# Strassen's seven products for three of the four gate pairs of the last branch

## The chip, the cores and the metric

The kernel runs on one core of a Trainium2 chip. The time is that of one execution in device microseconds; the figure of a kernel is the median of its runs. Matmuls run on TensorE (PE), which has an instruction stream of its own for loading weights (PEld); VectorE (DVE), ScalarE (ACT) and GpSimd (POOL) do the elementwise work, and SyncE (SP) issues the transfers.

## The reference

Two layers of a decoder trunk on x of 512 tokens by 1024 columns, float32. What matters here is the end of a layer:

```python
def hybrid_layer(x, ...):
    h = rms_norm(x, norm_g)
    proj = h @ w_in                      # (512, 1024) @ (1024, IN_COLS)
    ...                                  # three branches a, c, r, each (512, 512)
    g = jax.nn.sigmoid(gates).reshape(b, s, 3, 1024)
    merged = g[:, :, 0] * (a @ w_branch[0])
    merged = merged + g[:, :, 1] * (c @ w_branch[1])
    merged = merged + g[:, :, 2] * (r @ w_branch[2])
    return x + merged @ w_out
```

`gates` are the last 3 x 1024 columns of `proj`. The second layer is followed by a last RMSNorm.

## The kernel before

Everything is kept transposed: 128 features on the partitions, the 512 tokens along a row. The normalised input h is 8 such tiles, each as a high and a low part in a reduced float32 format (`split`, L196 to L198: ACT copies the high part on L197, DVE or POOL subtracts for the low part on L194). A product of full precision is three matmuls (`mm3`, L200 to L203: high by high L201, high by low L202, low by high L203).

Weights come as chunks of 128 x 1024 (512 KB), in an order fixed on the host (`chunk_order`). SP loads them into `wraw`, which has three buffers (L214); `split_next` splits a chunk into `whi` and `wlo` (three buffers each), ACT both halves, the low part of the first half on DVE and of the second on POOL. One chunk is split ahead of the one PE is using (`LOOK = 1`).

PE's order is that of the program text; the order of the other engines is set by a scheduler when the kernel is built. In the text, work that waits for other engines is put off by a count of `tick`s (`at(lag, fn)`), so that score blocks of attention and retention fall between projections.

`merge(br, parts, jp, first, final)` makes two of the 8 tiles of `merged` for one branch: one W chunk of the branch's weights and two gate chunks. For each of the two tiles `proj` makes the gate (8 weight tiles x 3 = 24 matmuls of 512 columns) and ACT its tanh (L489), then W gives 12 matmuls of 512 columns, DVE multiplies (L649, with the product in PSUM) and adds to the running sum m, a tile called xm (L650). For the last branch (`br == 2`, retention) the sum is split into `vm`, the operand of the output projection `out_proj`, whose first two output tiles take the operands 0 to 5 before the others. SP also reloads x into the buffers of xm (`xm<-xT`, `xm<-xsave`).

Retention runs between the merges of branch 0: `rk` and `rq` are rotated with the tables in the tile `tab` (L445 to L449), their low parts `qk` made on L461, a score block's diagonal multiplied by a triangle on L534, the block split into `st`, and PE multiplies it with the values (pa<-st,vm).

Of the kernel before, what the change touches and what calls it, by code (L numbers as in the profile page):

```python
# [38 lines left out]

def merge_chunks(br, jp):
    c = GATE + br * D + jp * 256
    return [("W", br, jp), ("A", c), ("A", c + P)]


# [26 lines left out]
    return L  # L73


def rot_perm(base):


    idx = []
    for h in range(4):  # L80
        for ihi in range(2):
            for half in range(2):
                for ilo in range(16):
                    idx.append(base + h * 64 + half * 32 + ihi * 16 + ilo)
    return idx


def lay_weights(w_in, w_branch, w_out):
    cols = np.arange(w_in.shape[2])
    cols[RQ:RQ + 256] = rot_perm(RQ)  # L90
    cols[RK:RK + 256] = rot_perm(RK)
    out = []
    for l in range(DEPTH):
        for c in chunk_order(l):
            if c[0] == "B":
                a = w_in[l][c[2] * 256:(c[2] + 1) * 256, c[1]:c[1] + 512].reshape(2, P, 512)
            elif c[0] == "A":
                a = w_in[l][:, cols[c[1]:c[1] + P]].reshape(8, P, P)
            elif c[0] == "W":
                a = w_branch[l, c[1]][:, c[2] * 256:(c[2] + 1) * 256].reshape(4, P, 256)  # L100
            else:
                a = w_out[l][:, c[1] * P:(c[1] + 1) * P].reshape(8, P, P)
            out.append(a.transpose(1, 0, 2).reshape(P, 1024))
    return np.stack(out)
# [50 lines left out]
def tile_hybrid_trunk(ctx: ExitStack, tc: tile.TileContext, xT, w, prm, lam, tab, cmat, outT):  # L155
# [29 lines left out]
    def pj():  # L185
        return ps.tile([P, S], F32, tag="pj", bufs=NPJ, name="pj")
# [16 lines left out]
        T.matmul(out, wl, xh, start=False, stop=stop)  # L203


    order = [(l, c) for l in range(DEPTH) for c in chunk_order(l)]
    pos = [0]
    raws, parts = [], []

    def prefetch():  # L210
        i = pos[0] + len(parts) + len(raws)
        if i < len(order):
            raw = t("wraw", 3, (P, 1024))
            nc.sync.dma_start(raw, w[i])  # L214
            raws.append(raw)

    def split_next():
        if not raws:
            prefetch()
        if raws:  # L220
            raw = raws.pop(0)
            l, c = order[pos[0] + len(parts)]
            off = 0 if c[0] == "O" and l == DEPTH - 1 else WOFF
            hi, lo = (tr(tag, 3, (P, WPITCH))[:, off:off + 1024] for tag in ("whi", "wlo"))
            for c in range(0, 1024, 512):
                c = slice(c, c + 512)
                if pos[0] or parts or c.start:
                    split(hi[:, c], lo[:, c], raw[:, c], G if c.start else V)
                else:
                    V.tensor_copy(hi[:, c], raw[:, c])  # L230
                    lo_part(lo[:, c], raw[:, c], hi[:, c])
            parts.append((hi, lo))

    def chunk(l, *key):

# [128 lines left out]
    for l in range(DEPTH):  # L364
# [269 lines left out]
        def merge(br, parts, jp, first, final):  # L634
            wh, wl = chunk(l, "W", br, jp)
            for i in range(2):
# [14 lines left out]
                if final:  # L651
                    hi, lo = tr("vm", 16), tr("vm", 16)
                    split(hi, lo, m[j])
                    mp[j] = (hi, lo)

        def attention(p):
            qk, o, wt = attn_qk(p), {}, {}
            for s in range(8):
                at(AOFF + ARATE * s, lambda s=s: attn_step(2 * p + s // 4, s % 4, o, wt, qk))
            for i in range(2):  # L660
                az[2 * p + i] = silu_proj(AZ + 256 * p + P * i)
# [12 lines left out]
        for jp in range(4):  # L674
            rz[jp] = silu_proj(RZ + P * jp)
            merge(0, abr, jp, False, False)
        assert len(abr) == 4 and len(rbr) == 4 and not todo, (len(abr), len(rbr), len(todo))
        for jp in range(4):
            merge(2, rbr, jp, False, True)


        x2 = []
# [80 lines left out]
```

## Time and profile before

| | before |
|---|---|
| median of 3 runs | 1064.31 us (1064.06 to 1064.67) |
| the profiled execution, its own time | 1063.46 us |
| its span, first to last instruction | 1061.7 us |
| mean granted clock of TensorE | 0.997 |
| busy PE / DVE / ACT / POOL | 1050.7 / 681.7 / 502.9 / 319.2 us |
| three last merge pairs of branch 2, layer 0 and 1 | 48.96 and 48.65 us |

The rows of the profile carry the line numbers of the kernel before. "Idle before" is the time in which an engine did nothing ahead of an instruction, with what ended it. Durations of neighbouring instructions on an engine overlap a little, so that the distance of starts is the better measure of the pace.

### The profile page before, as it was taken

What the parts mean: (1) busy time and instruction counts of PE and PEld (TensorE: products, weight loads), DVE (VectorE), ACT (ScalarE), POOL (GpSimd) and SP (SyncE); (2) the same over time, 40 slices, a digit from 0 to 9 for tenths busy, and PEclk for the clock granted to TensorE, in tenths of its full rate; (3) what the DMA queues carried; (4) which work ended last, traced back from release to release, by engine and by line L of the source; (5) the groups of instructions that cost most, each with busy time, mean ns of one, the idle gap of its engine ahead of it and who ended that gap; (6) DMA issues with size and microseconds to landing.
All of it is one profiled execution on the core that took longest, in us unless ns stands there. A gap on an engine that the chain in (4) does not pass through costs nothing.

```text
span 1061.7 us, 13847 instructions
## 1 busy us (share of the span) xinstructions
PE 1050.7 (99%) x5010; PEld 878.8 (83%) x5010; DVE 681.7 (64%) x1168; ACT 502.9 (47%) x942; POOL 319.2 (30%) x254
## 2 busy tenths in 40 slices
PE   8999999999999999999999999999999999999997
PEld 6888888888888888888888888888888888888896
DVE  7687686765677566345528776868546956654454
ACT  6454454543554555334434535545345545544343
POOL 6222233221233333232422222232112333332264
PEclk9999999999999999999999999999999999999998
DMA  6322222232234222444422232223313432134363
GB/s 253 107 96 99 84 76 86 93 119 80 80 119 139 66 91 79 132 129 146 143 100 90 80 119 79 81 80 108 111 61 100 135 100 78 65 107 132 110 208 121
DMA packets 34340, 113.57 MB, mean 107 GB/s; under 512 B 3936, under 2 KB 4064, under 8 KB 34272
## 3 DMA queue, kind: packets, MB, share of 16 engines
q1 hardware_dynamic: 34128, 112.44, 32.6%
q8 instruction: 39, 0.64, 0.2%
q14 instruction: 29, 0.24, 0.1%
q10 hardware_dynamic: 144, 0.26, 0.1%
HBM read 108.49 MB, written 4.19 MB: 106 GB/s over the span
## 4 chain that ended last, share of the span: by engine, by line
PE 92%; DVE 5%; ACT 1%; issue 1%; DMA 0%; SPq 0%; DVEq 0%; ACTq 0%
PE pj L201 28%; PE pj L203 28%; PE pj L202 28%; PE pa L479 3%; PE pa L203 1%; PE pa L202 1%; DVE wa L427 1%; PE pa L201 1%; DVE wlo L194 1%; PE pa L605 1%; DVE h L194 1%; DVE vm L395 1%; ACT h L197 1%; DMA xm<-xT 0%; DVE xb L375 0%
## 5 line engine op out<-in xcount | busy, mean ns | idle before, releaser
L194 POOL TENSOR_TENSOR wlo<-wraw,whi 128x512 fp32r<-128x512 f32 x184 | 252.1, 1372 | 626.6 <-ACT whi L197 584.5
L201 PE MATMUL pj<-h,whi 128*128 128x512 f32 x960 | 379.4, 395 | 0.0
L203 PE MATMUL pj<-h,wlo 128*128 128x512 f32 x960 | 374.9, 390 | 0.0
L202 PE MATMUL pj<-h,whi 128*128 128x512 f32 x960 | 374.3, 390 | 0.2
L197 ACT CAST whi<-wraw 128x512 fp32r<-128x512 f32 x367 | 216.4, 618 | 219.2 <-PE pj L202 144.8
L194 DVE TENSOR_TENSOR wlo<-wraw,whi 128x512 fp32r<-128x512 f32 x184 | 153.9, 837 | 125.4 <-ACT whi L197 124.3
L203 PEld LDWEIGHTS pj<-h,wlo 128*128 128x128 f32 x960 | 180.2, 188 | 39.3 <-DVE wlo L194 0.5
L202 PEld LDWEIGHTS pj<-h,whi 128*128 128x128 f32 x960 | 180.5, 188 | 35.7 <-DVE h L194 1.1
L201 PEld LDWEIGHTS pj<-h,whi 128*128 128x128 f32 x960 | 180.4, 188 | 35.0
L201 PE MATMUL pj<-xb,whi 128*128 128x512 f32 x192 | 75.1, 391 | 0.0
L203 PE MATMUL pj<-xb,wlo 128*128 128x512 f32 x192 | 74.8, 390 | 0.0
L202 PE MATMUL pj<-xb,whi 128*128 128x512 f32 x192 | 74.7, 389 | 0.0
L592 ACT ACTIVATE p<-pa,nm 128x128 f32<-128x128 f32 (+3 forms) x64 | 33.5, 526 | 69.0 <-DVE nm L589 68.8
L516 DVE RECIPROCAL e<-e 128x512 f32<-128x512 f32 x16 | 53.6, 3350 | 18.0 <-ACT e L515 18.0
L197 ACT CAST st<-pa 128x256 fp32r<-128x256 f32 (+2 forms) x80 | 29.7, 372 | 70.2 <-DVE pa L534 40.5
L201 PE MATMUL pj<-vm,whi 128*128 128x256 f32 (+1 forms) x192 | 60.5, 315 | 0.0
L202 PE MATMUL pj<-vm,whi 128*128 128x256 f32 (+1 forms) x192 | 60.4, 315 | 0.0
L203 PE MATMUL pj<-vm,wlo 128*128 128x256 f32 (+1 forms) x192 | 60.3, 314 | 0.0
L649 DVE SCALAR_TENSOR_TENSOR wb<-wa,pj 128x512 f32<-128x512 f32 x32 | 22.0, 687 | 41.8 <-PE pj L203 38.6
L194 DVE TENSOR_TENSOR st<-pa,st 128x256 fp32r<-128x256 f32 (+2 forms) x80 | 33.7, 421 | 17.0 <-ACT st L197 16.4
L203 PEld LDWEIGHTS pj<-xb,wlo 128*128 128x128 f32 x192 | 36.0, 188 | 7.6
L202 PEld LDWEIGHTS pj<-xb,whi 128*128 128x128 f32 x192 | 36.1, 188 | 7.2
(132 smaller groups left out, 1428.8 us busy)
## 6 DMA issues: line engine op xcount, KB each, us to landing
wraw<-w SPq DMA_DIRECT2D x183, 512.0 KB, 3.4
tab<-tab SPq DMA_DIRECT2D x10, 512.0 KB, 3.4
xm<-xT SPq DMA_DIRECT2D x15, 256.0 KB, 3.6
xsave<-xm SPq DMA_DIRECT2D x8, 256.0 KB, 2.1
xm<-xsave SPq DMA_DIRECT2D x8, 256.0 KB, 2.8
outT<-p SPq DMA_DIRECT2D x8, 256.0 KB, 2.1
wraw<-w SPq DMA_DIRECT2D x2, 256.0 KB, 3.3
xm<-xT ACTq DMA_DIRECT2D x1, 256.0 KB, 3.0
```

The source lines that it names most:

```text
L194: eng.tensor_tensor(lo, x, hi, op=ALU.subtract)
L197: A.copy(hi, x)
L201: T.matmul(out, wh, xh, start=start, stop=False)
L202: T.matmul(out, wh, xl, start=False, stop=False)
L203: T.matmul(out, wl, xh, start=False, stop=stop)
L395: V.scalar_tensor_tensor(lo, banks[tt], rtok[:, tt:tt + 1], hi, op0=ALU.mult, op1=ALU.subtract)
L427: V.scalar_tensor_tensor(hk, x[k], ng[k], rrow, op0=ALU.mult, op1=ALU.mult)
L479: T.matmul(o, ac[i][:, asl], bc[i][:, bsl], start=i == 0, stop=i == 1)
L516: V.reciprocal(r, r)
L592: A.activation(pc[:, :n], sp[:, :n], AF.Exp, bias=nm, scale=0.125, accum_out=sm)
L605: T.transpose(tp[:, j * P:(j + 1) * P], p1[:, j * P:(j + 1) * P], ident)
L649: V.scalar_tensor_tensor(y, g, 1.0, o, op0=ALU.add, op1=ALU.mult)
```

## The change

For branch 2 the pairs jp = 1, 2, 3 are made by `merge_fast`; jp = 0 stays as it was. The two gate tiles of a pair are a product of 2 x 2 blocks: two weight chunks a and b (128 gate columns each, each of two halves of 512, which are 4 of the 8 feature tiles), by h of two halves of features and two halves of tokens (LF and RT, 256 each). Instead of 8 products of quarters there are 7, in Winograd's form of Strassen's scheme, each of 4 feature tiles x 3 matmuls of 256 columns. It needs four sums of weights (`sources`: s1 = b0 + b1, s2 = s1 - a0, a0 - b0, a1 - s2; three on POOL, s2 on DVE), four sums of h (`h_sums` and `late_sums`, once in a layer, for kk = 0 to 3, with two 512-wide sums on POOL into the single buffer `tab`, four 256-wide ones on DVE, and two more splits), and seven additions of results on DVE instead of none (`add`), with one ACT copy out of PSUM. A pair's two chunks are used as four parts ("F"), which hold 3.5 x 1024 columns instead of 2 x 1024. `h_sums(0)` stands in the program behind the second merge of branch 0, the other three and `late_sums` ahead of the first merge of branch 2.

```diff
--- before.py
+++ after.py
@@ -39,8 +39,15 @@
 
 
 
+def fast(br, jp):
+    return br == 2 and jp > 0
 def merge_chunks(br, jp):
     c = GATE + br * D + jp * 256
+    if fast(br, jp):
+        return [("F", c), ("F", c + P), ("W", br, jp)]
     return [("W", br, jp), ("A", c), ("A", c + P)]
 
 
@@ -73,6 +80,18 @@
     return L
 
 
+def part_order(layer):
+    L, C = [], iter(chunk_order(layer))
+    for c in C:
+        if c[0] == "F":
+            next(C)
+            L += [("F", c[1], i) for i in range(4)]
+        else:
+            L.append(c)
+    return L
 def rot_perm(base):
 
 
...
@@ -203,33 +222,63 @@
         T.matmul(out, wl, xh, start=False, stop=stop)
 
 
-    order = [(l, c) for l in range(DEPTH) for c in chunk_order(l)]
-    pos = [0]
-    raws, parts = [], []
+    order = [(l, c) for l in range(DEPTH) for c in part_order(l)]
+    nchunks = sum(len(chunk_order(l)) for l in range(DEPTH))
+    pos, loaded = [0], [1]
+    raws, parts, fp = [], [], {}
 
     def prefetch():
-        i = pos[0] + len(parts) + len(raws)
-        if i < len(order):
+        if loaded[0] < nchunks:
             raw = t("wraw", 3, (P, 1024))
-            nc.sync.dma_start(raw, w[i])
+            nc.sync.dma_start(raw, w[loaded[0]])
+            loaded[0] += 1
             raws.append(raw)
 
-    def split_next():
+    def next_raw():
         if not raws:
             prefetch()
-        if raws:
-            raw = raws.pop(0)
-            l, c = order[pos[0] + len(parts)]
-            off = 0 if c[0] == "O" and l == DEPTH - 1 else WOFF
-            hi, lo = (tr(tag, 3, (P, WPITCH))[:, off:off + 1024] for tag in ("whi", "wlo"))
-            for c in range(0, 1024, 512):
-                c = slice(c, c + 512)
-                if pos[0] or parts or c.start:
-                    split(hi[:, c], lo[:, c], raw[:, c], G if c.start else V)
-                else:
-                    V.tensor_copy(hi[:, c], raw[:, c])
-                    lo_part(lo[:, c], raw[:, c], hi[:, c])
-            parts.append((hi, lo))
+        return raws.pop(0)
+    def sources(c):
+        if c[0] != "F":
+            raw = next_raw()
+            return [raw[:, 0:512], raw[:, 512:1024]]
+        if c[2] == 0:
+            ra, rb = next_raw(), next_raw()
+            fp["a"], fp["b"] = [[r[:, 0:512], r[:, 512:1024]] for r in (ra, rb)]
+        (a0, a1), (b0, b1) = fp["a"], fp["b"]
+        if c[2] == 0:
+            s1 = fp["s1"] = t("wc", 1)
+            G.tensor_tensor(s1, b0, b1, op=ALU.add)
+            return [a0, s1]
+        if c[2] == 1:
+            s2 = fp["s2"] = t("sq", 1)
+            V.tensor_tensor(s2, fp["s1"], a0, op=ALU.subtract)
+            return [a1, s2]
+        if c[2] == 2:
+            G.tensor_tensor(b0, a0, b0, op=ALU.subtract)
+            G.tensor_tensor(a1, a1, fp["s2"], op=ALU.subtract)
+            return [b0, a1]
+        return [b1]
+    def split_next():
+        n = pos[0] + len(parts)
+        if n == len(order):
+            return
+        l, c = order[n]
+        off = 0 if c[0] == "F" or c[0] == "O" and l == DEPTH - 1 else WOFF
+        src = sources(c)
+        hi, lo = (tr(tag, 3, (P, WPITCH))[:, off:off + 1024] for tag in ("whi", "wlo"))
+        for i, raw in enumerate(src):
+            c = slice(i * 512, i * 512 + 512)
+            if n or i:
+                split(hi[:, c], lo[:, c], raw, G if i else V)
+            else:
+                V.tensor_copy(hi[:, c], raw)
+                lo_part(lo[:, c], raw, hi[:, c])
+        parts.append((hi, lo))
 
     def chunk(l, *key):
 
@@ -653,6 +702,86 @@
                     split(hi, lo, m[j])
                     mp[j] = (hi, lo)
 
+        LF, RT = slice(0, 256), slice(256, 512)
+        hs, late = {}, {}
+        def h_sums(kk):
+            uv = t("tab", 1, (P, 2 * S))
+            u, v = uv[:, 0:S], uv[:, S:2 * S]
+            G.tensor_tensor(u, h[kk][0], h[kk][1], op=ALU.add)
+            G.tensor_tensor(v, h[4 + kk][0], h[4 + kk][1], op=ALU.add)
+            a, b = t("wc", 1), t(f"p{kk % 2}", 2)
+            V.tensor_tensor(a[:, LF], u[:, RT], u[:, LF], op=ALU.subtract)
+            V.tensor_tensor(a[:, RT], v[:, RT], a[:, LF], op=ALU.subtract)
+            V.tensor_tensor(b[:, LF], v[:, RT], u[:, RT], op=ALU.subtract)
+            V.tensor_tensor(b[:, RT], v[:, LF], a[:, RT], op=ALU.subtract)
+            hi, lo = tr("qk", 8), tr("qk", 8)
+            split(hi, lo, a)
+            hs[1, kk], hs[2, kk] = [(hi[:, s], lo[:, s]) for s in (LF, RT)]
+            late[kk] = b
+        def late_sums(kk):
+            hi, lo = tr("xb", 16), tr("xb", 16)
+            split(hi, lo, late[kk])
+            hs[3, kk], hs[4, kk] = [(hi[:, s], lo[:, s]) for s in (LF, RT)]
+        def quarter(o, part, i, mov):
+            for kk in range(4):
+                c = slice(i * 512 + kk * P, i * 512 + (kk + 1) * P)
+                mm3(o, part[0][:, c], part[1][:, c], *mov(kk), kk == 0, kk == 3)
+        def hq(k0, s):
+            return lambda kk: (h[k0 + kk][0][:, s], h[k0 + kk][1][:, s])
+        def ht(n):
+            return lambda kk: hs[n, kk]
+        def merge_fast(br, parts, jp):
+            c = GATE + br * D + jp * 256
+            ga, gb = t("ez", 4), t("ez", 4)
+            def quarters(n, moving):
+                p, o = chunk(l, "F", c, n), pa()
+                for i, mov in enumerate(moving):
+                    quarter(o[:, i * 256:(i + 1) * 256], p, i, mov)
+                return o[:, LF], o[:, RT]
+            def add(out, prod, other):
+                V.tensor_tensor(out, prod, other, op=ALU.add)
+            q1, q5 = quarters(0, (hq(0, LF), ht(1)))
+            A.copy(ga[:, LF], q1)
+            q2, q6 = quarters(1, (hq(4, LF), ht(2)))
+            u2 = t("e1", 1)
+            add(u2[:, LF], q6, ga[:, LF])
+            add(ga[:, LF], q2, ga[:, LF])
+            add(ga[:, RT], q5, u2[:, LF])
+            q7, q3 = quarters(2, (ht(3), hq(4, RT)))
+            add(gb[:, LF], q7, u2[:, LF])
+            add(ga[:, RT], q3, ga[:, RT])
+            tanh_half(ga, ga)
+            add(gb[:, RT], q5, gb[:, LF])
+            q4, _ = quarters(3, (ht(4),))
+            add(gb[:, LF], q4, gb[:, LF])
+            tanh_half(gb, gb)
+            wh, wl = chunk(l, "W", br, jp)
+            for i, g in enumerate((ga, gb)):
+                j, o = 2 * jp + i, pj()
+                for k in range(4):
+                    cs = slice(k * 256 + i * P, k * 256 + (i + 1) * P)
+                    mm3(o, wh[:, cs], wl[:, cs], parts[k][0], parts[k][1], k == 0, k == 3)
+                y = t("wb", 1)
+                V.scalar_tensor_tensor(y, g, 1.0, o, op0=ALU.add, op1=ALU.mult)
+                V.tensor_tensor(m[j], m[j], y, op=ALU.add)
+                hi, lo = tr("vm", 16), tr("vm", 16)
+                split(hi, lo, m[j])
+                mp[j] = (hi, lo)
         def attention(p):
             qk, o, wt = attn_qk(p), {}, {}
             for s in range(8):
@@ -674,9 +803,16 @@
         for jp in range(4):
             rz[jp] = silu_proj(RZ + P * jp)
             merge(0, abr, jp, False, False)
+            if jp == 1:
+                h_sums(0)
         assert len(abr) == 4 and len(rbr) == 4 and not todo, (len(abr), len(rbr), len(todo))
-        for jp in range(4):
-            merge(2, rbr, jp, False, True)
+        for kk in range(1, 4):
+            h_sums(kk)
+        for kk in range(4):
+            late_sums(kk)
+        merge(2, rbr, 0, False, True)
+        for jp in range(1, 4):
+            merge_fast(2, rbr, jp)
 
 
         x2 = []
```

In the order of the built kernels PE has 5161 rows instead of 4945, DVE 1120 instead of 1016 and POOL 180 instead of 124.

The first place is the start of retention in a layer, on DVE. Before (L461 makes qk's low parts, L534 is the triangle of a score block, `cm` holds the triangle, L649 and L650 belong to the merge of branch 0):

```order
L447 TENSOR_TENSOR wa<-pj,tab 128x512
L194 TENSOR_TENSOR wlo<-wraw,whi 128x512
L449 TENSOR_TENSOR wa<-wa,wb 128x512
L493 SCALAR_TENSOR_TENSOR ez<-ez,pj 128x512
L461 TENSOR_TENSOR qk<-wa,qk 64x512 x2
L194 TENSOR_TENSOR wlo<-wraw,whi 128x512
L534 TENSOR_TENSOR pa<-pa,cm 128x128
L194 TENSOR_TENSOR st<-pa,st 128x512
L649 SCALAR_TENSOR_TENSOR wb<-wa,pj 128x512
```

After the change the same stretch reads so (L496 is L447 of before, L510 L461, L542 L493, L583 L534; `p_3409` is the tile b of `h_sums(0)`, `p_3844` that of `h_sums(1)`, L718 to L721 are their four sums):

```order
L496 TENSOR_TENSOR wa<-pj,tab 128x512
L213 TENSOR_TENSOR wlo<-wraw,whi 128x512
L498 TENSOR_TENSOR wa<-wa,wb 128x512
L718 TENSOR_TENSOR wc<-tab 128x256
L720 TENSOR_TENSOR p_3409<-tab 128x256
L719 TENSOR_TENSOR wc<-tab,wc 128x256
L542 SCALAR_TENSOR_TENSOR ez<-ez,pj 128x512
L510 TENSOR_TENSOR qk<-wa,qk 64x512 x2
L721 TENSOR_TENSOR p_3409<-tab,wc 128x256
L720 TENSOR_TENSOR p_3844<-tab 128x256
L583 TENSOR_TENSOR pa<-pa,cm 128x128
L213 TENSOR_TENSOR wlo<-wraw,whi 128x512
```

Seven instructions more stand between L496 and the first triangle L583, the last of them L720 of the second chunk; a chunk's low part that stood ahead of the triangle now stands behind it.

POOL at the same place after the change, where L715 and L716 write `tab` for a chunk of h each and the other rows are second halves of weight chunks (before, only those were there):

```order
L213 TENSOR_TENSOR wlo<-wraw,whi 128x512
L715 TENSOR_TENSOR tab<-h 128x512
L716 TENSOR_TENSOR tab<-h 128x512
L213 TENSOR_TENSOR wlo<-wraw,whi 128x512
L715 TENSOR_TENSOR tab<-h 128x512
L716 TENSOR_TENSOR tab<-h 128x512
```

The two pairs of sums have one low part between them.

In a fast pair (the second of a layer) DVE has this after the change, where `sq<-wc,wraw` (L258) is s2 of the pair that follows, L755 are the additions of this pair, `wlo` the low parts of coming parts, L779 and L780 the merge (L649 and L650 before):

```order
L213 TENSOR_TENSOR wlo<-wraw,whi 128x512
L258 TENSOR_TENSOR sq<-wc,wraw 128x512
L755 TENSOR_TENSOR ez<-pa,e_4267 128x256
L755 TENSOR_TENSOR ez<-pa,ez 128x256 x2
L213 TENSOR_TENSOR wlo<-wraw,whi 128x512
L755 TENSOR_TENSOR ez<-pa,ez 128x256
L213 TENSOR_TENSOR wlo<-wraw,whi 128x512
L779 SCALAR_TENSOR_TENSOR wb<-ez,pj 128x512
L780 TENSOR_TENSOR xm<-xm,wb 128x512
L213 TENSOR_TENSOR vm<-xm,vm 128x512
L779 SCALAR_TENSOR_TENSOR wb<-ez,pj 128x512
```

L258 stands behind this pair's first three additions and ahead of its other four.

## Rows read from the trace of the kernel before

**Rows 1.** The page's head: span, and busy time of each engine

```profile
span 1061.7 us, 13847 instructions
...
PE 1050.7 (99%) x5010; PEld 878.8 (83%) x5010; DVE 681.7 (64%) x1168; ACT 502.9 (47%) x942; POOL 319.2 (30%) x254
```

**Rows 2.** Waits of PE: us in total, times, longest

```profile
PE pj L202 <- DVE wlo L194: 1.6, 2, 1.0
```

**Rows 3.** Windows: us; busy PE, PEld, DVE, ACT, POOL; clock, DMA share, GB/s

```profile
436.78:485.74 48.96, 48.96 (x218) 40.54 (x216) 21.42 (x27) 16.92 (x31) 12.28 (x10) 1.00 0.41 129
958.90:1007.55 48.65, 48.65 (x216) 40.27 (x215) 21.39 (x27) 16.60 (x31) 11.99 (x10) 1.00 0.41 130
```

**Rows 4.** A window of the last projection, and its timeline (start, us)

```profile
1022.00:1052.00 30.00, 30.00 (x265) 30.00 (x264) 14.05 (x29) 15.10 (x31) 21.41 (x20) 1.00 0.49 163
...
1007.55 0.28 PE L201 MATMUL pj<-vm,whi 128*128 128x256 f32 x1
...
1008.49 0.28 PE L203 MATMUL pj<-vm,wlo 128*128 128x256 f32 x1
```

**Rows 5.** Timeline of DVE and of POOL in a fast pair

```profile
454.57 1.78 DVE L650 TENSOR_TENSOR xm<-xm,wb 128x512 f32<-128x512 f32 x1
...
462.25 0.69 DVE L650 TENSOR_TENSOR xm<-xm,wb 128x512 f32<-128x512 f32 x1
...
454.29 1.52 POOL L194 TENSOR_TENSOR wlo<-wraw,whi 128x512 fp32r<-128x512 f32 x1 [0.85 <-ACT whi L197]
```

**Rows 6.** Groups of instructions: busy us, mean ns, idle before

```profile
L194 POOL TENSOR_TENSOR wlo<-wraw,whi 128x512 fp32r<-128x512 f32 x184 | 252.1, 1372 | 626.6 <-ACT whi L197 584.5 <-DVE h L194 13.0 <-DVE vm L395 8.3
L194 DVE TENSOR_TENSOR wlo<-wraw,whi 128x512 fp32r<-128x512 f32 x184 | 153.9, 837 | 125.4 <-ACT whi L197 124.3 <-issue 0.5 <-POOL wlo L194 0.2
L650 DVE TENSOR_TENSOR xm<-xm,wb 128x512 f32<-128x512 f32 x32 | 40.5, 1265 | 0.4
L649 DVE SCALAR_TENSOR_TENSOR wb<-wa,pj 128x512 f32<-128x512 f32 x32 | 22.0, 687 | 41.8 <-PE pj L203 38.6 <-ACT wa L489 3.2
L194 DVE TENSOR_TENSOR st<-pa,st 128x256 fp32r<-128x256 f32 x40 | 16.8, 421 | 8.3 <-ACT st L197 7.9
```

**Rows 7.** Timelines of DVE, ACT and PE at the start of retention, layer 0

```profile
326.71 0.68 DVE L447 TENSOR_TENSOR wa<-pj,tab 128x512 f32<-128x512 f32 x1
...
329.28 1.41 DVE L461 TENSOR_TENSOR qk<-wa,qk 64x512 fp32r<-64x512 f32 x2
...
332.43 0.28 DVE L534 TENSOR_TENSOR pa<-pa,cm 128x128 f32<-128x128 f32 x1
333.37 0.69 DVE L194 TENSOR_TENSOR st<-pa,st 128x512 fp32r<-128x512 f32 x1 [0.66 <-ACT st L197]
...
339.26 0.30 DVE L534 TENSOR_TENSOR pa<-pa,cm 128x128 f32<-128x128 f32 x1 [3.29 <-PE pa L479]
...
362.76 0.42 DVE L194 TENSOR_TENSOR st<-pa,st 128x256 fp32r<-128x256 f32 x1
363.10 0.68 DVE L649 SCALAR_TENSOR_TENSOR wb<-wa,pj 128x512 f32<-128x512 f32 x1
...
332.75 0.59 ACT L197 CAST st<-pa 128x512 fp32r<-128x512 f32 x1 [0.69 <-DVE pa L534]
...
335.38 0.40 PE L201 MATMUL pa<-st,vm 128*128 128x512 f32 x1
335.62 0.39 PE L202 MATMUL pa<-st,vm 128*128 128x512 f32 x1
```

**Rows 8.** The weight chunks' tile: issue ns, and issue to landing us

```profile
L214 SPq DMA_DIRECT2D wraw<-w x183: 327/328/610, 3.1 to 1040.7; - x183
...
DMA to landing us min/median/max: 3.1/3.4/6.6
```

**Rows 9.** A window behind PE's last work, and PE's first row

```profile
1056.00:1058.00 2.00, 0.00 (x0) 0.00 (x0) 2.00 (x6) 0.00 (x0) 0.00 (x0) 0.57 0.41 154
...
1.19 4.20 PE L279 MATMUL pa<-wb 128*128 128x512 bf16 x10 [1.19 <-DVE wb L274]
```

More of the change, by code (lines that the diff above doesn't have):

```diff
@@ L96, in lay_weights @@
                 a = w_in[l][c[2] * 256:(c[2] + 1) * 256, c[1]:c[1] + 512].reshape(2, P, 512)
-            elif c[0] == "A":
+            elif c[0] in "AF":
                 a = w_in[l][:, cols[c[1]:c[1] + P]].reshape(8, P, P)
```

## Prediction

> **What bounds the kernel now.** I read the page's head first: PE works through 1050.7 of a span of 1061.7 us, DVE 64%, POOL 30% [rows 1]. Then the waits of PE: the longest there is comes to 1.6 us over the whole run [rows 2]. So time falls only where PE gets less to do, and it rises wherever PE is made to wait for something that comes in time today. Then the stage that is changed. PE goes through its six pairs without a gap: the first layer's three take 48.96 us, 16.32 each, the second one's 48.65; 216 weight loads in 48.96 us give 0.2267 us for a product 512 columns wide; DVE is busy 21.42 us of it, 7.14 a pair, POOL 12.28, or 4.09 a pair, and the clock is full [rows 3].
>
> **Taken away: products.** A pair's two gate tiles are 48 products of 512 columns today, 48 x 0.2267 = 10.88 us. Afterwards they are 7 quarters x 4 chunks x 3 = 84 products of 256 columns. What one of those takes the trace has in the last projection: 30.0 us for 265, or 0.1132 each, a little under half of 0.2267 [rows 4]. A slower pace occurs there too, 0.1175 (nine starts from 1007.55 to 1008.49, eight steps) [rows 4]. So 84 x 0.1133 = 9.52 us, a gain of 1.36 a pair and **8.16 us** over six pairs; at 0.1175 it would be 9.87, or 6.1 us. I take the first, which holds for nearly all of those 30 us. The merge's own 24 products a pair stay (5.44 us), so a pair would take 9.52 + 5.44 = 14.96 us.
>
> **Added: sums on DVE and POOL, and what they cost by meeting.** DVE takes 0.69 us for a sum of two 512-column tiles in SBUF when POOL is still, and 1.78 us for the same line when POOL is in the middle of an instruction: L650 started at 454.57, POOL's 1.52 us had begun at 454.29, and DVE came free about 0.54 us after POOL did [rows 5]. Over the run L650 averages 1265 ns, while L649, which has one operand in PSUM, keeps 687 [rows 6]. So it is not width but two operands in SBUF beside a running POOL. The Trainium skill says so as a rule (SBUF — State Buffer, Who interferes with whom): a DVE instruction with two SBUF inputs contends with a GpSimd instruction that reads SBUF, and whichever has the port first blocks the other wholly. It speaks against this change, and rows 5 and 6 agree with it; by it the two waits below would lie at their upper ends, without it at their lower ones.
>
> The change sets such sums on both engines. In a pair POOL gets s1, b0 and a1 beside the four halves it splits: 7 x 1.37 = 9.6 us of 14.96, against 4.09 of 16.32 [rows 3, 6]. DVE gets s2 and seven adds 256 wide, which read PSUM and so don't meet (0.42 us, as the 256-wide split that reads PSUM [rows 6]).
>
> **First place, the start of retention.** This is once in each layer. Today DVE runs from L447 at 326.71 to the triangle of the first score block at 332.43, the ACT copy follows at 332.75, DVE's low part at 333.37, and PE takes the high part at 335.38 and the low one at 335.62: the low part, ready at 334.06, is 1.56 us early [rows 7]. Afterwards h_sums(0) and the first half of h_sums(1) stand in DVE's queue ahead of that triangle (the order excerpts of the first place). Their two buffers are in the tile "tab", which has one buffer: POOL can begin only when L447 has read the table (327.39), two sums of 1.29 end at 330.0; DVE makes its four (0.34 apart, as 362.76 and 363.10 show [rows 7]), among them the standing ez step (0.60) and the two qk low parts (1.4), and is done at about 333.0; only then may POOL write the second chunk's two sums, until 335.6; DVE's L720 needs the second of these, and the triangle stands behind L720: so the triangle starts at 335.95 instead of 332.43. From its start to the end of the low part it takes 1.63 us today, which gives 337.6 in place of the 335.62 at which PE wants it. That is 2.0 us of waiting on PE with no collision. With them (L718 and L720 each wait for POOL's running sum, the qk low parts meet the split of a chunk, POOL itself goes from 1.29 to 1.52) the triangle comes at about 338, the low part at 339.8: 4.2 us. I take the middle, 3.1 a layer, **6.2 us**. What is late next is the second score block, behind the same queue, but PE then has its full chain of gate and retention products, so I charge it nothing. The later chunks' sums (kk 2 and 3) and the eight splits cost nothing by the same reckoning: they lie under the merge of branch 0, where PE is full and DVE is idle for 3.29 us in one piece ahead of 339.26 [rows 7]; without that cover each chunk would be 2.6 us of POOL and 2 us of DVE on the path.
>
> **Second place, the fast pairs.** Here is a loop. The last quarter's low part p3 (DVE) frees the buffer that holds chunk b; only then can SP send for the next b, 0.33 us to issue and 3.4 us to landing [rows 8]; then POOL's s1 (1.3), then DVE's s2, which stands in DVE's queue ahead of the adds of q7, q3 and q4 (the order excerpt of the pair); behind them come two low parts of the next quarters, STT, the merge sum, vm, twice, and p3 again. With no meetings that makes 3.4 + 0.3 + 1.3 + 0.7 + 4 adds and 2 STT at 0.33 to 0.6 (2.5) + eight low parts and merge sums at 0.6 (4.8) + two ACT copies (1.2) = 14.2 us, just below PE's 14.96: no wait. Of the ten instructions on DVE with two SBUF inputs a pair, nine are in the loop, beside a POOL that is busy 64% of the time instead of 25%. Over the run the excess of such instructions is (32 x 0.58 + 184 x 0.15) / 216 = 0.21 us at POOL's 30% (1265 and 837 ns against 0.69) [rows 6]; scaled to 64% that is 0.45, so a loop of up to 18.2. Following the queues row by row with a wait wherever POOL is running, I get a loop near 17.5 and PE held at four places a layer: 0.9 at the merge chunk of the second pair, 0.55, 1.1 and 1.0 at the first and third quarter and the merge chunk of the third pair, 3.55 together; the first pair has its chunks in time. The ends are 0 and 3.55; I take 3.0 a layer, **6.0 us**, near the upper end, because rows 5 show the meeting as what happens whenever POOL is under way. xm's loads stand on SP behind vm and shift with it; they are needed only in the projection.
>
> **Last**, in the second layer vm of the last tile is the projection's eighth operand and comes later by the tail of that loop: **0.3 us**, between 0 and 0.4.
>
> **Sum**: -8.16 + 6.2 + 6.0 + 0.3 = +4.3 us. The profiled execution took 1063.46 us, 1061.7 of it span; the median of the runs is 1064.31, 0.85 above it. The difference carries over: 1064.31 + 4.3 = 1068.6 us. A measurement of this kernel can tell about 0.2%, 2.1 us.
>
> **Rivals.** *The meetings cost little (faster).* If DVE's sums mostly fall into POOL's gaps, the second place costs nothing and the first 2.0: -8.16 + 4.0 = -4.16, 1060.2 us. It decides when both places together cost under 3.0 us a layer. For it: the wlo low parts average 837 ns, so most go free today [rows 6], and the loop without meetings fits by 0.8 us. Against it: POOL has more than twice the work. *The waits just eat the gain*: 2.0 at the first place, 2.0 to 2.5 at the second, 1064 to 1065. *The clock falls in the wait of the first place.* The trace shows that it can: full in all stages, 0.57 in the two us from 1056 in which PE does nothing [rows 9]; and the ten first products of the run took 0.42 us each against 0.2267, 1.9 us lost [rows 9]. Twice 1.9 on top: 1072.4 us; with both places at their upper ends 1076. Against it: PE's wait is 4.2 us at the most and is broken by single products. The Trainium skill (TensorE: Matmul & The Clock Gate, Why this matters for your kernels) asks that no idle gaps be left between bursts of matmuls, since the throughput drops in mid-kernel; no wait of this trace is long enough to show it. *The narrow products don't run at half the time*: with 0.1175 the gain is 6.1, but a pair then takes 15.31 us and waits less for the loop of 17.5, by some 1.05 us a layer: 1068.6 again, so this changes the rows and hardly the time.
>
> **How the numbers follow.** Forecast as above, 1066.5 to 1071.5: 0.48. Meetings cost little, 1059 to 1062: 0.18. Waits eat the gain, 1062.2 to 1066.4: 0.20. Clock falls, 1071.5 to 1076: 0.12. Something else: 0.02. The range 1060.3 to 1074.5 leaves out a piece of the second and of the fourth. Faster 0.18, same 0.20, slower 0.62. The forecast alone would be 1066.5 to 1071.5.
>
> **What the profile will show.** Products of 256 columns from qk, xb and h at 0.113 us and some 9.5 us a gate pair in the first fast pair; a wait of PE of 2 to 4.2 us at the first retention block of each layer, ended by DVE's or ACT's st, with the triangle behind L720 behind POOL's L716; waits in the second and third fast pair but not in the first, ended by wlo; L780 and s2 well above 0.69 us on average; POOL above 60% busy there. I am wrong if the triangle comes before POOL's second pair of sums, if a fast pair takes 15.0 us three times over, or if PE waits at a place not named here.

## The result and the profile after

The changed kernel takes 1081.32 us (median of 4 runs, 1080.29 to 1082.22) against 1064.44 us before: 1.0159 times as long, 95% interval 1.0141 to 1.0176. It is slower, as forecast, but by 16.9 us instead of 4.3, and 1081.3 lies above the range (1074.5). Lines below are those of the changed kernel: L213 is L194 of before, L220 to L222 are L201 to L203, L583 is L534.

The page's head ([rows 1] before): DVE has 75 us more to do, POOL 61, and PE, with fewer columns to work through, 4 us more.

```profile
span 1079.1 us, 14473 instructions
...
PE 1055.0 (98%) x5226; PEld 888.2 (82%) x5226; DVE 757.0 (70%) x1276; ACT 522.5 (48%) x982; POOL 380.6 (35%) x294
```

The waits of PE ([rows 2] before), us in total, times, longest:

```profile
PE pa L220 <- ACT st L216: 8.5, 2, 4.3
PE pa L222 <- DVE wlo L213: 2.7, 3, 1.2
PE pj L221 <- DVE wlo L213: 1.4, 2, 1.2
```

The first line is the first retention product of each layer. Timelines of DVE, POOL and PE there ([rows 7] before):

```profile
329.86 1.52 DVE L718 TENSOR_TENSOR wc<-tab 128x256 f32<-128x256 f32 x1
...
334.60 0.43 DVE L721 TENSOR_TENSOR p<-tab,wc 128x256 f32<-128x256 f32 x1
337.70 1.47 DVE L720 TENSOR_TENSOR p<-tab 128x256 f32<-128x256 f32 x1 [2.67 <-POOL tab L716]
339.09 0.28 DVE L583 TENSOR_TENSOR pa<-pa,cm 128x128 f32<-128x128 f32 x1
...
340.02 0.69 DVE L213 TENSOR_TENSOR st<-pa,st 128x512 fp32r<-128x512 f32 x1
...
327.72 1.67 POOL L715 TENSOR_TENSOR tab<-h 128x512 f32<-128x512 f32 x1 [5.25 <-DVE wa L496]
329.34 1.74 POOL L716 TENSOR_TENSOR tab<-h 128x512 f32<-128x512 f32 x1
...
335.17 1.28 POOL L715 TENSOR_TENSOR tab<-h 128x512 f32<-128x512 f32 x1 [1.87 <-DVE p L721]
336.39 1.27 POOL L716 TENSOR_TENSOR tab<-h 128x512 f32<-128x512 f32 x1
337.61 1.27 POOL L213 TENSOR_TENSOR wlo<-wraw,whi 128x512 fp32r<-128x512 f32 x1
...
340.05 0.50 PE L220 MATMUL pa<-st,vm 128*128 128x512 f32 x1 [4.25 <-ACT st L216]
...
341.78 0.63 PE L220 MATMUL pj<-h,whi 128*128 128x512 f32 x1
342.20 0.63 PE L221 MATMUL pj<-h,whi 128*128 128x512 f32 x1
...
345.69 0.28 PE L528 MATMUL pa<-qk 128*128 128x256 f32 x1
```

Before, the second score block followed the products at 335.38 [rows 7] here:

```profile
338.83 0.28 PE L479 MATMUL pa<-qk 128*128 128x256 f32 x1
```

POOL's second pair of sums waits for L721, L720 waits 2.67 us for POOL and then meets the split that POOL began at 337.61 (1.47 us for a sum that takes 0.41), and the triangle L583 comes behind it. It starts 6.66 us later than before. PE starts its retention products at 340.05 instead of 335.38, and the next score block (L528) follows 5.64 us later instead of 3.45. The windows show the clock meanwhile (the last three numbers are clock, DMA share and GB/s):

```profile
335.00:338.00 3.00, 0.80 (x4) 0.33 (x2) 0.33 (x2) 0.77 (x2) 2.83 (x3) 1.00 0.30 122
338.00:341.00 3.00, 0.73 (x2) 0.42 (x3) 2.94 (x5) 0.58 (x1) 0.89 (x1) 0.97 0.00 0
341.00:344.00 3.00, 3.00 (x8) 2.33 (x9) 1.62 (x4) 0.48 (x1) 0.00 (x0) 0.50 0.49 175
```

The clock is halved just when PE has work again: its products of 512 columns then start 0.43 us apart (341.78 and 342.20) instead of 0.23. A part of the 5.64 us is not the clock: the low part `st`, which DVE begins at 340.02, is late for PE's second product, too. Experiment 2 parts the two.

The same happens once more in each layer, ahead of a head norm (L561 and L562 are its products with `ones_p`). The last chunk's L720 waits for POOL and then meets the split that POOL has just begun, and a triangle stands behind it:

```profile
376.80 1.29 POOL L716 TENSOR_TENSOR tab<-h 128x512 f32<-128x512 f32 x1
378.05 2.72 POOL L213 TENSOR_TENSOR wlo<-wraw,whi 128x512 fp32r<-128x512 f32 x2
...
378.12 1.50 DVE L720 TENSOR_TENSOR p<-tab 128x256 f32<-128x256 f32 x1 [2.71 <-POOL tab L716]
...
380.14 0.28 DVE L583 TENSOR_TENSOR pa<-pa,cm 128x128 f32<-128x128 f32 x1
```

That triangle was at 369.39 before and is 10.75 us later, while PE is only 6.9 us later there. ACT's copies come behind it, and the low parts of the block and of the norm reach PE late (at 382.58 and 383.62): 0.8 us in each layer.

The three fast pairs of each layer ([rows 3] before), and DVE's p3 and s2 in the first layer:

```profile
444.44:492.23 47.79, 46.59 (x326) 43.17 (x324) 37.36 (x56) 22.87 (x42) 29.84 (x20) 1.00 0.44 142
972.95:1022.42 49.47, 47.19 (x325) 43.20 (x324) 37.40 (x55) 22.66 (x42) 29.86 (x20) 1.00 0.43 137
```

```profile
449.61 0.69 DVE L213 TENSOR_TENSOR wlo<-wraw,whi 128x512 fp32r<-128x512 f32 x1
...
455.29 0.69 DVE L258 TENSOR_TENSOR sq<-wc,wraw 128x512 f32<-128x512 f32 x1 [3.12 <-POOL wc L254]
...
466.74 0.68 DVE L213 TENSOR_TENSOR wlo<-wraw,whi 128x512 fp32r<-128x512 f32 x1
...
472.47 0.69 DVE L258 TENSOR_TENSOR sq<-wc,wraw 128x512 f32<-128x512 f32 x1 [2.63 <-POOL wc L254]
...
483.94 0.68 DVE L213 TENSOR_TENSOR wlo<-wraw,whi 128x512 fp32r<-128x512 f32 x1
```

(Before, the second layer's three pairs begin at 958.59 and so take 48.96 us like the first layer's; the window of [rows 3] starts 0.31 us late.) From p3 to p3 it is 17.13 and 17.20 us, from s2 to s2 17.18: the loop. And the pace of the narrow products, first and last of a pair's 84 (83 steps in 9.77 us, 0.1177 each):

```profile
444.44 0.28 PE L220 MATMUL pa<-h,whi 128*128 128x256 f32 x1
...
454.21 0.28 PE L222 MATMUL pa<-xb,wlo 128*128 128x256 f32 x1
```

Laid side by side, PE's starts before and after give the account (its last product starts 16.9 us later):

| term, both layers | forecast | measured |
|---|---|---|
| gate products | -8.2 | -5.9 (84 x 0.1177 = 9.89 instead of 10.88, six times) |
| waits in the fast pairs | +6.0 | +5.2 (47.79 and 49.47 less 46.02 without waits) |
| start of retention: wait | +6.2 | +8.8 (4.43 + 4.38) |
| behind it, up to the second score block | 0 | +4.9 (2.19 + 2.69; by experiment 2 half clock 3.7, late low part 1.2) |
| rest of retention (head norms) | 0 | +1.6 |
| last projection | +0.3 | +2.0 |
| elsewhere | 0 | +0.3 |
| sum | +4.3 | +16.9 |

### The profile page after: what moved, and what is told of

Same layout as the page of the kernel before. It is cut to its first block, busy times and chain, and to the rows that moved or that the text cites. A ratio compares the mean times of both kernels' runs of the same rounds, so it can differ in the third digit from the quotient of the medians.

```text
span 1079.1 us, 14473 instructions
## 1 busy us (share of the span) xinstructions
PE 1055.0 (98%) x5226; PEld 888.2 (82%) x5226; DVE 757.0 (70%) x1276; ACT 522.5 (48%) x982; POOL 380.6 (35%) x294
## 5 line engine op out<-in xcount | busy, mean ns | idle before, releaser
L213 POOL TENSOR_TENSOR wlo<-wraw,whi 128x512 fp32r<-128x512 f32 x178 | 245.1, 1380 | 528.3 <-ACT whi L216 483.7
L220 PE MATMUL pj<-h,whi 128*128 128x512 f32 x864 | 343.3, 397 | 0.0
L222 PE MATMUL pj<-h,wlo 128*128 128x512 f32 x864 | 338.5, 392 | 0.0
L221 PE MATMUL pj<-h,whi 128*128 128x512 f32 x864 | 338.1, 391 | 0.2
L216 ACT CAST whi<-wraw 128x512 fp32r<-128x512 f32 x373 | 219.4, 618 | 169.1 <-PE pj L221 77.0
L213 DVE TENSOR_TENSOR wlo<-wraw,whi 128x512 fp32r<-128x512 f32 x196 | 172.1, 879 | 70.5 <-ACT whi L216 69.6
L222 PEld LDWEIGHTS pj<-h,wlo 128*128 128x128 f32 x864 | 162.9, 189 | 35.8 <-DVE wlo L213 0.5
L221 PEld LDWEIGHTS pj<-h,whi 128*128 128x128 f32 x864 | 163.2, 189 | 32.2 <-DVE h L213 1.1
L220 PEld LDWEIGHTS pj<-h,whi 128*128 128x128 f32 x864 | 163.3, 189 | 31.6
L222 PE MATMUL pj<-xb,wlo 128*128 128x512 f32 x192 | 75.1, 391 | 0.8 <-DVE wlo L213 0.8
L220 PE MATMUL pj<-xb,whi 128*128 128x512 f32 x192 | 75.1, 391 | 0.0
L221 PE MATMUL pj<-xb,whi 128*128 128x512 f32 x192 | 74.8, 389 | 0.0
L221 PE MATMUL pj<-vm,whi 128*128 128x256 f32 (+1 forms) x192 | 60.7, 316 | 0.3 <-DVE vm L213 0.3
L220 PE MATMUL pj<-vm,whi 128*128 128x256 f32 (+1 forms) x192 | 61.0, 318 | 0.0
L222 PE MATMUL pj<-vm,wlo 128*128 128x256 f32 (+1 forms) x192 | 60.6, 316 | 0.0
L213 DVE TENSOR_TENSOR st<-pa,st 128x256 fp32r<-128x256 f32 (+2 forms) x80 | 33.5, 419 | 15.6 <-ACT st L216 15.1
L222 PEld LDWEIGHTS pj<-xb,wlo 128*128 128x128 f32 x192 | 36.0, 188 | 9.7 <-DVE wlo L213 2.1
L221 PEld LDWEIGHTS pj<-xb,whi 128*128 128x128 f32 x192 | 36.1, 188 | 6.9
L220 PEld LDWEIGHTS pj<-xb,whi 128*128 128x128 f32 x192 | 36.1, 188 | 6.8
```

The costliest lines, as they stand in the source:

```text
L213: eng.tensor_tensor(lo, x, hi, op=ALU.subtract)
L216: A.copy(hi, x)
L220: T.matmul(out, wh, xh, start=start, stop=False)
L221: T.matmul(out, wh, xl, start=False, stop=False)
```

## The experiments

**1. All sums of h behind the last triangle.** `tc.issue_after(ins)` sets DVE's instructions of a block behind `ins` in its queue.

```diff
-            if jp == 1:
-                h_sums(0)
...
-        for kk in range(1, 4):
-            h_sums(kk)
+        with tc.issue_after(tris[-1].ins):
+            for kk in range(4):
+                h_sums(kk)
```

> All four h_sums are queued on DVE behind the last triangle of retention, so that no triangle stands behind a sum. The theory (the triangle queued behind L720, which waits for POOL's second pair of sums in the one buffer tab; PE then waits 4.25 us and goes on at half its clock): PE's wait at the first retention block is gone, the clock stays at 1.00 there, and the 7.4 and 7.9 us that the two layers lose between the start of retention and the first fast pair go: 1081.3 - 15.3 = 1066.0 us. The rival (the sums' work itself is too much for DVE and POOL wherever it stands): the wait comes up elsewhere in the merges of branch 0, and the time stays above 1078 us.

Measured: 1091.43 us, 1.0251 times before (1.0236 to 1.0267): slower still, and clock 0.987. The wait at the first retention block is gone, but others stand at the last head's norm and in the merges behind it:

```profile
PE pj L222 <- DVE wlo L213: 8.0, 5, 3.6
PE pa L562 <- POOL st L213: 5.9, 2, 3.0
```

POOL's timeline shows how:

```profile
413.09 1.29 POOL L715 TENSOR_TENSOR tab<-h 128x512 f32<-128x512 f32 x1 [2.41 <-DVE p L721]
414.34 1.72 POOL L716 TENSOR_TENSOR tab<-h 128x512 f32<-128x512 f32 x1
416.01 1.71 POOL L213 TENSOR_TENSOR wlo<-wraw,whi 128x512 fp32r<-128x512 f32 x1
417.69 1.44 POOL L213 TENSOR_TENSOR st<-sq,st 128x512 fp32r<-128x512 f32 x1
```

POOL waits for DVE to free `tab`, and the low part `st` for which PE waits stands behind. So the forecast of 1066.0 was wrong and the rival's sign came (above 1078), and "the sums have no room anywhere" became a rival to be taken seriously; experiment 5 decides it.

**2. Products to fill the wait.** In each layer, ahead of the first retention product:

```diff
+FILL = 18
...
+                if hd == 0 and j == 0:
+                    fp_ = pa()
+                    for f in range(FILL):
+                        T.matmul(fp_, h[0][0][:, 0:P], h[0][0], start=True, stop=True)
                 mm3(o[hd][:, qs], rv[j][0][:, vs], rv[j][1][:, vs], sh[:, :n], sl[:, :n], j == 0, j == 3)
```

> The changed kernel with 18 more products of 512 columns (results unused, 4.1 us at full clock) on PE ahead of the first retention product of each layer; the queue of DVE is as it was. The theory that the loss behind the wait is the clock: the products lie inside the 4.25 us, the granted clock stays at 1.00 behind them, and 2 x 2.2 us come back: about 1076.9 us. The rival that the loss behind the wait is late score blocks and not the clock: no gain, 1081 us or more, with the clock at 1.00 and the same distance from the first retention product to the second score block.

Measured: 1075.42 us, 5.9 us less than the changed kernel, though PE has 36 products more. The first retention product still starts late, at 339.81, but the next score block follows 4.06 us behind it instead of 5.64, at full clock (its line numbers are one higher: L221 is L220 of the changed kernel):

```profile
339.81 0.50 PE L221 MATMUL pa<-st,vm 128*128 128x512 f32 x1 [0.24 <-ACT st L217]
...
343.87 0.28 PE L529 MATMUL pa<-qk 128*128 128x256 f32 x1
...
341.00:344.00 3.00, 3.00 (x16) 2.44 (x15) 1.39 (x4) 0.59 (x2) 0.00 (x0) 1.00 0.42 154
```

In the second layer it is 4.05 us instead of 6.14. So the half clock costs 1.6 and 2.1 us, 3.7 together; the other 0.6 us a layer (4.06 against 3.45 before) stays at full clock and belongs to the low part, for which PE still waits 0.22 us. The rest of the 5.9 us is mostly in the second layer's fast pairs, 48.0 us instead of 49.5, and in the last projection; why the waits there changed was not followed.

**3. No weight sums.**

```diff
-            return [a0, s1]
+            return [a0, b0]
...
-            return [a1, s2]
+            return [a1, b1]
```

and the sums s1, s2 and both sums in place left out.

> The four sums of weight chunks are left out (the raw quarters take their place, so the gate values are other numbers); products, additions of results and sums of h stay. The theory of the loop (load of b, s1 on POOL, s2 on DVE ahead of the additions, 17.2 us against 15.34 of PE): the third pair of each layer comes down from 17.1 and about 18 us to 15.34, the waits of 1.8 and 3.4 us go, 1081.3 - 5.2 = 1076.1 us, POOL back to about 4 us a pair. The rival (the loop is the load and the three buffers, not the sums): less than 2 us.

Measured: 1074.54 us, 6.8 less; PE does not wait in the pairs, which take three times 15.34 us in both layers:

```profile
444.41:490.43 46.02, 46.02 (x325) 43.19 (x324) 33.63 (x54) 22.75 (x42) 19.87 (x13) 1.00 0.46 147
970.41:1016.43 46.02, 46.02 (x325) 43.19 (x324) 33.17 (x54) 22.85 (x42) 19.10 (x13) 1.00 0.45 147
```

So the 5.2 us of waits in the pairs go with the weight sums. The other 1.6 us stand elsewhere: about 0.8 at the second layer's start of retention, where the clock is back at 1.00 sooner, and the rest mostly in the last projection, where PE no longer waits for vm.

**4. Eight quarters.** The kernel before, its six pairs' gates in two halves of 256 tokens:

```diff
+                for q in halves:
+                    for k in range(NK):
+                        c = slice(k * P, (k + 1) * P)
+                        mm3(o[:, q], wh[:, c], wl[:, c], h[k][0][:, q], h[k][1][:, q], k == 0, k == NK - 1)
```

> The kernel before, with the gates of the same six pairs made in two halves of 256 tokens, 96 products of 256 columns a pair instead of 48 of 512, no sums. If products of 256 columns run at 0.1178 us in this stretch whatever their operands are: 96 x 0.1178 - 10.88 = 0.43 us a pair, +2.6 us, 1067.0 us. If they run at 0.1133 and the 0.1178 of the changed kernel is due to its operands (sums in qk and xb, results in pa): no change, 1064.4 us.

Measured: 1068.67 us, 1.0038 times before (1.0023 to 1.0052). A tile is 0.34 us longer than before (8.50 instead of 8.16 from start to start), and its products start 0.1200 us apart. Neither number was met, but the sign is settled: in this stretch narrow products cost more than half, with ordinary operands too.

**5. The sums spread.** `h_sums(kk)` behind triangle 4 kk + 1:

```diff
+        for kk in range(4):
+            with tc.issue_after(tris[4 * kk + 1].ins):
+                h_sums(kk)
```

> As the changed kernel, but h_sums(kk) stands on DVE behind triangle 4 kk + 1 of retention (no triangle of the first two blocks stands behind a sum, and POOL never waits long for L721 to free tab). The theory (what costs is the place in the two queues: a sum of one engine waiting for the other engine with other work behind it): no wait of PE in retention nor, as with all sums at the end, in the merges behind it, clock 1.00: 1081.3 - 15.3 = 1066 us. The rival (the work of the sums, about 2.6 us of POOL and 2 us of DVE each, finds no room anywhere): waits come up at other score blocks, 1075 us or more.

Measured: 1065.59 us, 1.0004 times before (0.9995 to 1.0013), 15.7 us less than the changed kernel: no measurable difference from before. The same work costs PE nothing at these places: ahead of the fast pairs PE is 0.1 us behind the kernel before in the first layer, and no further behind in the second layer's retention. The waits that PE still has in the fast pairs and the projection:

```profile
PE pa L222 <- DVE wlo L213: 3.1, 3, 1.4
PE pj L220 <- ACT vm L216: 0.9, 1, 0.9
PE pj L222 <- DVE wlo L213: 0.5, 2, 0.3
```

**6. s2 on POOL.** `V.tensor_tensor(s2, ...)` becomes `G.tensor_tensor(s2, ...)`.

> As the changed kernel, but s2 is made by POOL behind s1, so that DVE's additions of q7, q3 and q4 no longer stand behind the load of b and s1. Theory of the loop: the third pair of each layer comes down to 15.34 us, as it did without any weight sums (-5.2 in the pairs, -6.8 in the whole): 1074.5 to 1076 us. The rival: POOL, with eight instructions a pair (10.4 us at 1.3, 13.9 at the 1.74 that it takes beside DVE), becomes the bound; then the pairs stay at 17 us and it is 1081 us or more.

Measured: 1083.42 us, 1.0169 (1.0154 to 1.0184), not faster than the changed kernel. DVE's waits in the pairs are gone, POOL's stand there, and vm is late for the projection:

```profile
PE pa L222 <- POOL wlo L213: 3.3, 2, 1.8
PE pj L220 <- ACT vm L216: 2.2, 1, 2.2
```

The rival holds: the third pair still takes 17.7 and 17.4 us, and the wait is now for POOL, which makes the sum. Behind the last of these waits the clock is at 0.59 and 0.56 for four us.

**7. u and v on DVE.** The two `G.tensor_tensor` of `h_sums` become `V.tensor_tensor`.

> As the changed kernel, but u and v of h_sums are made by DVE (0.6 us each instead of POOL's 1.3), so that DVE and POOL don't wait for each other in turn; the sums of h_sums(0), and only these, stand ahead of the first triangle. Theory of the turns: the first triangle is late by 2 x 0.6 + 4 x 0.34 = 2.6 us, its low part by 1.0 us for PE, the clock holds: 4.25 + 2.2 - 1.0 = 5.4 us less a layer, 1070.5 us. The rival (it is DVE's load there, not the turns): the wait stays near 4 us, 1080 us.

Measured: 1069.10 us, 1.0037 (1.0025 to 1.0050), near the 1070.5 expected. PE waits 1.55 us at the first retention block instead of 4.25, and the page's mean clock is back at 0.997:

```profile
PE pa L221 <- DVE st L213: 3.1, 2, 1.6
```

More work for DVE, and less wait, so DVE's load is not the matter. The edit does two things, though: the engines no longer wait for each other in turn, and the second chunk's L720 now stands behind the first triangle. The run does not part them.

**8. 5 and 6 together.**

> Both together: sums of h spread behind the triangles, s2 on POOL. If both theories hold, the terms add: 1081.3 - 15.3 - 5.2 to 6.8 = 1059 to 1061 us, under the kernel before (1064.8 on that chip). If the sums' work has no room, 1070 us or more.

Measured: 1065.37 us, 1.0005 (0.9996 to 1.0015): the gain of 5, nothing from 6; the forecast of 1059 to 1061 was missed.

**9. The loop shortened.** The second tile's STT, merge sum and vm behind p3 of the next pair, on top of 5:

```diff
             q7, q3 = quarters(2, (ht(3), hq(4, RT)))
+            while held:
+                with tc.issue_after(fp["last"].ins):
+                    held.pop(0)()
```

> As the run with the sums of h spread behind the triangles, and the second tile's STT, merge sum and vm of a fast pair are queued on DVE behind p3 of the next pair, so that chunk b's buffer comes free about 2.8 us earlier. Theory of the loop (17.2 us from p3 to p3, of which these instructions are about 2.8): the loop falls to about 14.4, under PE's 15.34; the pairs take 15.34 us each, the 2.0 and 3.1 us that they wait in the two layers with the sums spread go: 1065.6 - 5.1 = 1060.5 us. The rival (s2 and the additions wait for POOL and the load, whatever stands behind them, as with s2 on POOL): less than 2 us, 1064 to 1066.

Measured: 1062.40 us against 1064.79, ratio 0.9977 (0.9968 to 0.9987): with experiment 10, which builds on it, the only one below the kernel before. It lies between the two forecasts (1060.5, and 1064 to 1066). From s2 to s2 it is now 15.98 us instead of 17.18, not 14.4:

```profile
447.90 0.69 DVE L258 TENSOR_TENSOR sq<-wc,wraw 128x512 f32<-128x512 f32 x1 [3.14 <-POOL wc L254]
...
463.88 0.69 DVE L258 TENSOR_TENSOR sq<-wc,wraw 128x512 f32<-128x512 f32 x1 [1.18 <-POOL wc L254]
```

The pairs take 46.84 and 47.84 us, so that half of their waits is gone (48.2 and 49.1 us in 5); what they still wait for is W's low part, behind the moved instructions.

**10. The same with a small product ahead of each pair.**

> The same with one product of 64 columns (result overwritten) ahead of each fast pair's first quarter. The spacing of 256-column products has been 0.1178 or 0.1133 in one and the same program, and changed only where PE had waited or had other work. If what stands just ahead of a stretch sets the spacing, the small product can bring the pairs to 0.1133 (84 x 0.0045 = 0.38 us a pair, -2.3 us for six); if it is bound to the operands, the spacing stays at 0.1178 and the time at the other run's plus 0.2 us or so.

Measured: 1063.25 us, 0.9984 (0.9975 to 0.9992). The spacing stayed at 0.1178 in all six pairs.

**11. The sums of h alone.** `fast()` returns False and `merge` makes all pairs, the sums stay.

> One part of the change alone: the sums of h (h_sums, late_sums) are made where the changed kernel makes them, but nothing uses them; all gates are made as before, in products of 512 columns. If the start of retention is the whole loss, with its wait of 4.25 us, the half clock behind it (2.2 to 2.7 us) and 0.8 us at the head norms, this is 1064.8 + 15.3 = 1080 us, about as slow as the changed kernel. If the loss needs the fast pairs, too (their loads, their order), it is nearer 1065 to 1070 us.

Measured: 1084.85 us, 1.0186 (1.0171 to 1.0202). The first retention block waits 4.25 us in each layer as in the changed kernel, so the fast pairs have no part in it. The 5 us above the forecast are a place of its own: with other work around it the scheduler set two pairs of sums ahead of a head norm's `st` on POOL. PE waits 2.47 us there in each layer, with the half clock behind it, and loses 4.3 us where the changed kernel loses 0.8 (in the profiled execution, 1087.70 us, the longest of the four):

```profile
PE pa L220 <- ACT st L216: 8.5, 2, 4.2
PE pa L562 <- POOL st L213: 4.9, 2, 2.5
```

**12. The held instructions one step later,** behind W's low part.

> As the run with the second tile's STT, merge sum and vm behind p3 of the next pair, but they are queued one step later, behind the low part of the merge chunk W, which PE still waited for there (0.34, 0.66 and 0.57 us). If the place in DVE's queue is what makes W late, these waits go and the pairs come near 46.0 us a layer instead of 46.8 and 47.8: 1062.4 - 2.0 = 1060.4 us. The rival: the held instructions now stand beside s2 and the next pair's first parts and make these late instead: 1062.4 us or more.

Measured: 1067.08 us, 1.0018 (1.0008 to 1.0029). The rival's number came (1062.4 or more), its place only in part: the first layer's pairs fall to 46.5 us, the second's stay at 47.8, with a wait of 1.07 us for the third pair's first part. And vm, which neither forecast had named, now comes 2.24 us late for the last projection; behind that wait the clock is halved once more:

```profile
1010.00:1012.00 2.00, 0.00 (x0) 0.00 (x0) 1.34 (x2) 0.62 (x1) 0.19 (x1) 1.00 0.39 119
...
1014.00:1016.00 2.00, 2.00 (x11) 2.00 (x11) 1.68 (x3) 2.00 (x5) 1.49 (x2) 0.50 0.32 124
```

## Why the prediction was wrong

**First place, the step that failed.** "I take the middle, 3.1 a layer" of the ends 2.0 and 4.2, with "the clock falls in the wait of the first place" as a rival at 0.12. The place, the queue and the mechanism were right: triangle behind L720 behind POOL's second pair. The size was over the upper end: 4.4 a layer to the first product and 4.9 to the second one, which needs the low part that the forecast reckoned with. Nearly all the meetings that the upper end counts happened: L715 1.67, L716 1.74, L718 1.52, L720 1.47 us; only POOL's second pair of sums went free (1.28 and 1.27). And the clock fell in both layers, 1.6 and 2.1 us by experiment 2. That was priced well (1.9 a layer from [rows 9]) but held for unlikely on the ground that single products break the wait; they did not, PE stood still for 4.25 us in one piece. Wait, half clock, late low part and head norms are 15.3 us where 6.2 stood; experiment 5 takes all of it away, 2 shows the clock's part. "The later chunks' sums (kk 2 and 3) and the eight splits cost nothing" missed the 1.6 us at the head norms: there the last chunk's L720 holds up a triangle just as the second chunk's does at the start. In 1 and 11 it is another queue: POOL's sums stand ahead of the norm's `st`.

**Gate products.** "I take the first [0.1133], which holds for nearly all of those 30 us" was wrong: all 504 ran at 0.1177 (but for the waits), and in experiment 4 at 0.1200. The gain is 5.9, not 8.16. Nor did the better pace hold for nearly all of the 30 us: 5.6 of them, from 1035.39 on, ran at 0.1178. The forecast took a spacing from another stretch of the program and its better one; the rows held the other one, too. The rival on this said that the slower pace hardly changes the time, since the loop sets the pairs; that is borne out only in part: the gain is 2.3 us less and the waits 0.8, so that the two together came to -0.7 us against the -2.2 of the forecast.

**Second place.** Right in mechanism and size: a loop of "near 17.5" measured 17.1 to 17.2, waits of 6.0 measured 5.2, in the third pair mostly, and it is the weight sums that make it: without them the waits go whole (3), with a shorter loop by half (9). One detail was off: in the loop s2 did not meet POOL (0.69 us four times; only the first pairs' took 1.78), and POOL's L261 was the slow one beside it (1.80 us, 1742 ns on average over all six). And the loop without meetings, 14.2, was not reached by taking 2.8 us from it.

**Last projection.** 0.3 forecast, 2.0 measured: vm late by some 0.6 us, and the projection's products, which ran at 0.1133 in most of the stretch before, at 0.1178 after.

**The side of the range.** With both places at their upper ends and the clock down as well, 1076 had been worked out; the range stopped short of it, since that case held only a part of 0.12. It came, and the late low part, the slower products of the gates and the projection, and the head norms on top of it.

## What to carry to other kernels

A sum made by one engine for another in a single buffer makes the two queues wait in turn, and what stands behind the waiting instruction pays: look in the built order for what PE needs behind each such wait, and give the sums places where nothing urgent follows. The same work cost 15.7 us at one place and nothing at another. Where a forecast has two ends because of collisions, and a wait may cost the clock as well, give the case in which both happen a chance of its own: here the half clock stood behind the waits of 4.25 us, and it was gone where they were filled (2) or cut to 1.55 us (7).

## What the runs showed of the hardware

Products of 256 columns have two spacings, 0.1133 and 0.1178 us, in one program with the same operands, and a third, 0.1200, in experiment 4, all at a granted clock of 1.00. In the kernel before, the last projection went from 0.1178 to 0.1133 at 1012.26, at one step of 0.22 us, back to 0.1178 at 1035.39 and to 0.1133 again at 1041.27, the last two times behind a few narrower products; after the change it stayed at 0.1178 through longer waits. In experiments 1, 5, 7, 8 and 12 stretches within a fast pair ran at 0.1133, in 5 and 7 some 45 products behind one wait of PE, and it was 0.1178 again behind the next. A small product ahead did not change it (10). What chooses between them stays open.

The clock went to its lower level (0.50, 1.2 GHz) behind PE's waits of 4.25 us in both layers, behind the waits for vm of 2.17 us in experiment 6 and 2.24 us in 12, and behind those of 2.47 us in 11 and 2.96 and 3.57 us in 1; it stayed at the higher one (1.00, 2.4 GHz) behind 2.04 us in 8 and 1.55 us in 7. Products without use held it up (2).

An instruction of DVE with both inputs in SBUF took far longer when it began beside a running POOL instruction: a sum of 256 columns (L718, L720) 1.5 us instead of 0.41. The additions with one input in PSUM (L755, as wide) kept 0.41 us on average, though POOL was busy for 62% of the first layer's fast pairs.
